# First modulation block split into two halves of 128 channels, context tiles and tables loaded elsewhere, in a one-core diffusion backbone kernel

## Chip, cores and metric

The kernel runs on one core of a Trainium2 chip. The metric is the device time of one execution in microseconds (us), lower is better. All data is float32; the large matrix products take their operands as pairs of a rounded part and a remainder ("H" and "L" tiles) and add three products of them.

## What is computed

Two layers over 256 latent tokens `x` and 256 context tokens `ctx`, with 2048 channels each. The part that matters here is the entry of the first layer: every token row is normalised, then scaled and shifted by vectors that come from a matrix product with the conditioning vector, and the result is multiplied with the columns of the input projection.

```python
def rms_norm(x, g):
    y = x * rsqrt(mean(x * x, -1) + 1e-6)
    return y * g
m = silu(cond) @ ada_w + ada_b            # 2048 -> 3 * 2048
shift, scale, gate = split(m, 3)
h  = rms_norm(x,   g) * (1 + scale)   + shift      # latent rows, cond = c
hc = rms_norm(ctx, g) * (1 + scale_c) + shift_c    # context rows, cond = c_ctx
p, pc = h @ w_in, hc @ w_in[:, keys and later]     # q, gates, z, k, v, xBC, dt
# then neighbourhood attention + two-way state space scan, output projection,
# residual with the gate; second layer: the same kind of entry, a gated short
# convolution between two projections, residual with its gate
```

## The kernel before

The program is one long instruction list. It is written out while a planner (class `Plan`, lines 38 to 133) keeps an estimated finishing time for each engine and tile; generators hand in pieces of work, and `pump` (278) and `force` (299) decide from these estimates which piece is written next. On the chip each engine then runs its instructions strictly in that order. `pump` looks through the lists `urgent`, `side` and `back`, takes the first task in the list that `may` go (246), and starts again from the top of the list, so that in `urgent` a task that was spawned earlier goes first as long as its turn is possible.

Weights come in chunks of 128 x 1024 (512 KB) through a set of raw buffers: five named `raw`, and during the entry four more (`PT` twice, `xtm`, `yi`; line 181). `loads` is the fixed order of the loads, all issued on SyncE's queue by `issue` (365) as raw buffers come free. A chunk is rounded on ScalarE (line 420) and its remainder taken on VectorE (line 427) into one of three places; `use` and `used` hand these to the matrix products.

The entry has eight blocks of 256 channels, j = 0 to 7. For each block `ada_gen` (702) computes scale and shift: four 512 KB chunks of `ada0` for each of the two, 16 matmuls of 128 x 256 for each (line 718), a copy to SBUF (724), two transposes (728), a reduction and one or two small additions on VectorE (732 to 738). Then the two 128-channel tiles of normalised, transposed tokens (`xm`) are turned into `hH` (ScalarE, 757) and `hL` (VectorE, 759 and 763). For block 0 the weight chunk of the keys is rounded in two halves by `split_half` (436), one for each channel tile. Tokens are loaded by `x_load` (578), 128 rows at a time: t = 0 and 1 are latent rows, t = 2 and 3 context rows. Rows 2 and 3 go into the tiles `KT` and `KL`, in which rows 0 and 1 stood before. `x_norm` (594) computes the row sums and scales the rows; `x_pair` (617) transposes two channel tiles and copies them out of PSUM, one on ScalarE (628), one on VectorE (629). `x_gen(0)` is the first task in `urgent`, `ada_gen` the second, `x_gen(1)` the third.

The main loop (870) starts with block 0: keys of t = 0, 1 (12 matmuls for both channel tiles), then values (12), then queries (12), then keys and values of t = 2 and of t = 3, then the B columns (`b_part`). Blocks 1 to 7 follow in the same way, for all rows at once. `rows_` and `kv` (848, 859) issue these products.

Two tables, the rest of `small` (170 KB) and of `const` (224 KB), are loaded right after the context rows (lines 533, 534). `gemv_gen` (812), on the list `back`, computes further modulation vectors on VectorE from `adaT` chunks; it needs the conditioning vector as a row broadcast to all partitions, in the tile `csb`. Its loads share the raw buffers from the end of the entry on (`later_loads`, 505).

Of the kernel before, what the change touches and what calls it, by code (L numbers as in the profile page):

```python
# [14 lines left out]
D = 2048  # L15
KB = 16
# [125 lines left out]
def kernel(ctx: ExitStack, tc, x, cx, ada0, w0, adaT, w_in, w_out, sc_in, sc_out, rpb, small, const,  # L142
# [32 lines left out]
    QT, Vt, gt = st([128, 4, 256], "QT", F32R), st([128, 4, 512], "Vt"), st([128, 4, 256], "gt")  # L175
    xrow.append(st([128, D], "KL", name="x1"))
    QL = st([128, 4, 256], "QL", F32R)
# [351 lines left out]
    q_ada(0)  # L529
    w_seg(0, CK, CV, CQ)  # L530
    loads.append(lambda: x_load(2))
    loads.append(lambda: x_load(3))
    loads.append(lambda: E(DMA.dma_start(sm[:, NFIRST:], small[:, NFIRST:])))
    loads.append(lambda: E(DMA.dma_start(cs_[:, CFIRST:], const[:, CFIRST:])))
    weight(w_in, 0, 2, COL_B, 256)
    q_ada(1)
    for j in range(1, 8):
        w_seg(j, CK, CV)
        if j < 7:
            q_ada(j + 1)  # L540
        w_seg(j, CQ)
        weight(w_in, j * 256, 2, COL_B, 256)
    loads.append(later_loads)
# [31 lines left out]
    XS = {}  # L575
    ssq = st([128, 16], "ssq")

    def x_load(t):
        src = x if t < 2 else cx
        r0 = (t % 2) * 128  # L580
        xt = xrow[t] if t < 2 else st([128, D], ("KT", "KL")[t % 2], name=f"x{t}")
        for q in range(0, 4, 2):
            E(DMA.dma_start(xt[:, q * 512:(q + 2) * 512], src[r0:r0 + 128, q * 512:(q + 2) * 512]))  # L583
            XS[4 * t + q], XS[4 * t + q + 1] = (xt[:, p * 512:(p + 1) * 512] for p in (q, q + 1))

# [47 lines left out]
    def x_gen(c):  # L633
# [6 lines left out]
        for k2 in range(c, KB // 2):  # L640
            yield from x_pair(k2, ts)
# [60 lines left out]
    def ada_gen():  # L702
        bc = lambda ap: ap.unsqueeze(2).to_broadcast([128, 2, 2])
        for j in range(8):
            k2 = slice(2 * j, 2 * j + 2)
            for part, dst in ((0, A0), (1, S0)):
                ps = None
                for q in range(4):
                    key = ("ada", j, part, q)
                    w_ = 2 if j == 0 else 4  # L710
                    if q % w_ == 0:
                        ks = [("ada", j, part, q + i) for i in range(w_)]
                        yield when(lambda: all(k in RAW for k in ks))
                        yield W_("PE", *[RAW[k][1] for k in ks], nb=0 if ps is not None else 1)
                    if ps is None:
                        ps = bank()
                    raw, v = RAW.pop(key)
                    for g in range(4):
                        mm(ps[32 * g:32 * g + 32, :256], cpad[:, 4 * q + g, :], v[:, g, :], q == 0, q == 3)
                    give_raw(raw)  # L720
                    issue()
                yield W_("ACT", ps)
                Rt = half()
                E(S.copy(Rt, ps[:, :256]))

                yield W_("PE", Rt)
                for b in range(2):
                    turn(ps[:, 256 + b * 128:384 + b * 128], Rt[:, b * 128:(b + 1) * 128])
                give(free_h, Rt)
                yield W_("DVE", ps)  # L730
                p2 = dst[:, k2, :]
                E(V.tensor_reduce(out=p2, in_=ps[:, 256:].rearrange("p (b g c) -> p b c g", b=2, c=32)[:, :, 0:2, :],
                                  axis=AX.X, op=ALU.add))
                if part == 0:
                    E(V.tensor_tensor(out=dst[:, k2, :], in0=p2, in1=bc(bs1[:, k2]), op=ALU.add))
                    E(V.tensor_tensor(out=dst[:, k2, :], in0=dst[:, k2, :], in1=bc(g0[:, k2]), op=ALU.mult))
                else:
                    E(V.tensor_tensor(out=dst[:, k2, :], in0=p2, in1=bc(P_("ab0")[:, k2]), op=ALU.add))
                give(free_b, ps)

            for ts in ((0, 1), (2,), (3,)) if j == 0 else ((0, 1, 2, 3),):
                yield when(lambda: all(("xm", t, j) in got for t in ts))
                spans = [(k, slice(max(256 * k, 128 * ts[0]), min(256 * k + 256, 128 * ts[-1] + 128)))
                         for k in range(2) if {2 * k, 2 * k + 1} & set(ts)]
                o = slice(128 * ts[0], 128 * ts[-1] + 128)
                for kb in (2 * j, 2 * j + 1):
                    if j:

                        yield when(lambda: need[0] >= j or plan.t["DVE"] <= plan.t["PE"] + 600)
                    yield W_("DVE", xnT[kb][:, o])  # L750
                    hf = tmp()
                    if hH[kb] is None:
                        hH[kb] = st([128, 512], f"hH{kb}", F32R, name=f"hH{kb}")
                    if ts == (0, 1):
                        split_half(kb)
                    for k, ok_ in spans:
                        E(S.activation(hH[kb][:, ok_], xnT[kb][:, ok_], AF.Identity, scale=A0[:, kb, k:k + 1],  # L757
                                       bias=S0[:, kb, k:k + 1]))
                        E(V.tensor_scalar(out=hf[:, ok_], in0=xnT[kb][:, ok_], scalar1=A0[:, kb, k:k + 1],
                                          scalar2=S0[:, kb, k:k + 1], op0=ALU.mult, op1=ALU.add))  # L760
                    if hL[kb] is None:
                        hL[kb] = st([128, 512], f"hL{kb}", F32R, name=f"hL{kb}")
                    E(V.tensor_tensor(out=hL[kb][:, o], in0=hf[:, o], in1=hH[kb][:, o].bitcast(F32), op=ALU.subtract))  # L763
                    give(free_t, hf)
                    if ts == (0, 1):
                        halfsplit.pop()()
                if ts == (0, 1):
                    hold[0] = False
                    split()
                    split()  # L770
                got.update(("h", j, t) for t in ts)
# [26 lines left out]
    rowt = st([128, 128], "rowt")  # L798
    n_back = [0]
# [12 lines left out]
    def gemv_gen():  # L812
        yield from rows_out(csil[:, 0:KB], crow[0])
# [1239 lines left out]
```

## Time and profile before

| what | value |
|---|---|
| time, median of 3 runs | 1763.3 us (1760.74 to 1771.8) |
| time of the profiled execution | 1760.31 us |
| its span, first to last instruction | 1758.5 us |
| TensorE busy | 1736.7 us, 99% of the span |
| VectorE busy | 1223.6 us, 70% |
| ScalarE busy | 773.4 us, 44% |
| granted TensorE clock, mean | 0.999 |
| moved by DMA | 377.66 MB, mean 215 GB/s |

The profile lists busy time by engine, by group of instructions and by window of time; PE is TensorE, PEld its weight load, DVE VectorE, ACT ScalarE, POOL GpSimd, SPq the queue of SyncE that issues the loads. A timeline row gives start, duration, engine, line, operation, tiles and count, and in brackets how long the engine had been idle and what ended that. "Idle" of TensorE is what decides here, since it is busy nearly all the time.

### The profile page before, as it was taken

What the parts mean: (1) busy time and instruction counts of PE and PEld (TensorE: products, weight loads), DVE (VectorE), ACT (ScalarE), POOL (GpSimd) and SP (SyncE); (2) the same over time, 40 slices, a digit from 0 to 9 for tenths busy, and PEclk for the clock granted to TensorE, in tenths of its full rate; (3) what the DMA queues carried; (4) which work ended last, traced back from release to release, by engine and by line L of the source; (5) the groups of instructions that cost most, each with busy time, mean ns of one, the idle gap of its engine ahead of it and who ended that gap; (6) DMA issues with size and microseconds to landing.
All of it is one profiled execution on the core that took longest, in us unless ns stands there. A gap on an engine that the chain in (4) does not pass through costs nothing.

```text
span 1758.5 us, 25025 instructions
## 1 busy us (share of the span) xinstructions
PE 1736.7 (99%) x9451; PEld 1463.1 (83%) x9451; DVE 1223.6 (70%) x1978; ACT 773.4 (44%) x1330; POOL 31.6 (2%) x28
## 2 busy tenths in 40 slices
PE   6999999999999999999999999999999999999998
PEld 4777988889888889888888898888888888888887
DVE  5666887878685878686877787787668555555554
ACT  5333544445242436343435343564446444444442
POOL 0000100001000000000000000000000000000000
PEclk9999999999999999999999999999999999999999
DMA  9987644686756767656776557768767666666563
GB/s 362 342 307 258 209 143 138 183 246 191 234 165 195 219 205 227 210 175 210 220 213 193 166 185 255 246 221 284 274 222 228 195 188 192 192 191 188 190 208 121
DMA packets 202536, 377.66 MB, mean 215 GB/s; under 512 B 32384, under 2 KB 69040, under 8 KB 202416
## 3 DMA queue, kind: packets, MB, share of 16 engines
q1 hardware_dynamic: 195152, 369.49, 65.5%
q10 hardware_dynamic: 7264, 6.58, 1.1%
q8 instruction: 74, 1.21, 0.3%
q14 instruction: 46, 0.38, 0.1%
HBM read 370.62 MB, written 6.71 MB: 215 GB/s over the span
## 4 chain that ended last, share of the span: by engine, by line
PE 94%; DMA 2%; DVE 2%; issue 1%; ACT 0%; POOL 0%; SPq 0%; ACTq 0%; DVEq 0%; POOLq 0%
PE bank L195 91%; PE bank L199 3%; DMA tmp<-dram_csr 1%; DVE w L427 1%; DMA raw<-in_ada 0%; DMA tmp<-dram_exr 0%; DMA raw<-in_adaT 0%; DVE tmp L1235 0%; ACT w L420 0%; POOL statk L572 0%; DVE mix L1562 0%; SPq L583 0%; DVE raw L823 0%; DVE tmp L603 0%; DVE Vt L1012 0%
## 5 line engine op out<-in xcount | busy, mean ns | idle before, releaser
L420 ACT CAST w<-raw 128x1024 fp32r<-128x1024 f32 x343 | 359.5, 1049 | 530.4 <-PE bank L195 447.7
L427 DVE TENSOR_TENSOR w<-raw,w 128x1024 fp32r<-128x1024 f32 x343 | 416.6, 1217 | 231.4 <-ACT w L420 230.1
L195 PE MATMUL bank<-hH,w 128*128 128x256 f32 (+1 forms) x2064 | 488.0, 324 | 1.2 <-DVE w L427 1.1
L195 PE MATMUL bank<-w,hH 128*128 128x512 f32 x1280 | 407.4, 396 | 2.7 <-ACT hH L757 2.5
L195 PEld LDWEIGHTS bank<-hH,w 128*128 128x128 f32 x2064 | 344.7, 188 | 34.2 <-DVE w L427 2.1
L195 PE MATMUL bank<-hL,w 128*128 128x256 f32 (+1 forms) x1040 | 334.3, 321 | 0.0
L195 PEld LDWEIGHTS bank<-w,hH 128*128 128x128 f32 x1280 | 237.7, 189 | 54.4 <-issue 4.0
L195 PE MATMUL bank<-w,hL 128*128 128x512 f32 x640 | 249.9, 391 | 0.1
L195 PEld LDWEIGHTS bank<-hL,w 128*128 128x128 f32 x1040 | 196.3, 189 | 14.9
L195 PE MATMUL bank<-w,h 128*128 128x512 f32 x768 | 179.7, 390 | 0.0
L823 DVE CUSTOM_DVE_ANT_0 raw<-raw,csb 128x1024 f32<-128x1024 f32 x128 | 155.4, 1219 | 26.2 <-DMA raw<-in_adaT 24.0
L195 PEld LDWEIGHTS bank<-w,h 128*128 128x128 f32 x768 | 143.6, 188 | 29.6
L195 PEld LDWEIGHTS bank<-w,hL 128*128 128x128 f32 x640 | 120.5, 188 | 25.4 <-DVE hL L763 0.6
L195 PE MATMUL bank<-w,mix 128*128 128x512 f32 x588 | 138.3, 391 | 0.9 <-DVE w L427 0.9
L195 PEld LDWEIGHTS bank<-w,mix 128*128 128x128 f32 x588 | 109.5, 188 | 24.0 <-DVE w L427 1.3
L1235 DVE SCALAR_TENSOR_TENSOR tmp<-bank,cwh,tmp 128x508 f32<-128x508 f32 (+1 forms) x96 | 71.0, 744 | 1.8
L195 PE MATMUL bank<-KL,h 128*128 128x512 f32 x264 | 63.8, 389 | 0.0
L427 DVE TENSOR_TENSOR KL<-raw,KL 128x1024 fp32r<-128x1024 f32 x32 | 39.1, 1223 | 33.1 <-ACT KL L420 33.1
L427 DVE TENSOR_TENSOR wL<-raw,wH 128x1024 fp32r<-128x1024 f32 x31 | 37.9, 1224 | 33.5 <-ACT wH L420 33.4
L427 DVE TENSOR_TENSOR QL<-raw,QT 128x1024 fp32r<-128x1024 f32 x32 | 39.2, 1224 | 29.8 <-ACT QT L420 29.8
L195 PEld LDWEIGHTS bank<-KL,h 128*128 128x128 f32 x264 | 49.5, 188 | 10.2
L195 PE MATMUL bank<-QT,h 128*128 128x512 f32 x168 | 56.2, 391 | 0.0
(291 smaller groups left out, 1984.7 us busy)
## 6 DMA issues: line engine op xcount, KB each, us to landing
raw<-in_w_in SPq DMA_DIRECT2D x196, 512.0 KB, 3.9
raw<-in_adaT SPq DMA_DIRECT2D x128, 512.0 KB, 4.8
raw<-in_sc_in SPq DMA_DIRECT2D x128, 512.0 KB, 3.8
raw<-in_w_out SPq DMA_DIRECT2D x64, 512.0 KB, 5.0
raw<-in_ada SPq DMA_DIRECT2D x34, 512.0 KB, 6.9
raw<-in_sc_out SPq DMA_DIRECT2D x32, 512.0 KB, 4.1
PT<-in_ada SPq DMA_DIRECT2D x16, 512.0 KB, 6.9
raw<-in_w SPq DMA_DIRECT2D x16, 512.0 KB, 6.1
```

Of the source, the lines that this page charges most:

```text
L195: E(T.matmul(o, l, r, start=start, stop=stop, skip_group_check=True))
L199: E(T.transpose(o, i, ident if k == 128 else ident[:k, :k]))
L420: E(S.copy(H, v))
L427: E(V.tensor_tensor(out=Lo, in0=v, in1=H.bitcast(F32), op=ALU.subtract))
L823: E(V.tensor_tensor_reduce(out=raw, in0=raw, in1=csb, scale=1.0, scalar=0.0, op0=ALU.mult, op1=ALU.add, accum_out=gp[:, h, m:m + 1]))
L1235: E(V.scalar_tensor_tensor(out=do, in0=di, scalar=cwh[:, 32 * k + ch:32 * k + ch + 1], in1=do, op0=ALU.mult, op1=ALU.add))
```

## The change

Block 0 is cut into its two 128-channel tiles. Its eight `ada0` chunks are repacked on the host so that four of them hold all that channel tile 0 needs and four all that tile 1 needs (each chunk is now 8 x 128 rows by 128 columns). Their loads stand around the key and value chunks: four for tile 0, keys, values, four for tile 1, queries. The matmuls for them are 128 x 128, 64 in place of 32 of 128 x 256. The main loop issues keys and values of tile 0 as soon as tile 0 is modulated, then waits for tile 1 and issues the rest.

The transposes of the latent rows beyond the first pair (`x_pair` with k2 from 1) wait until the transposed shift of tile 1 has been written out (`("mm", 1, 1)`).

Context rows go to places that are free from the start: row tile 2 to `QT` and `QL`, row tile 3 to `csb` and to `hH14` and `hH15`. As `csb` is taken until then, `gemv_gen` starts only when the entry is over (`("V", 0)`). The two tables are loaded after block 3's chunks. `split_half` now enters the key chunk as split after its first half, and gives the raw buffer back after the second.

```diff
+    xhalf = [st([128, 1024], "QT", name="x2a")]
+    xhalf.append(st([128, 1024], "QL", name="x2b"))
...
             if b:
                 RAW.pop(0)
+                give_raw(raw)
+                issue()
+            else:
                 place()
                 HL[0] = (H, Lo)
                 pos["split"] += 1
-                give_raw(raw)
-                issue()
...
-    q_ada(0)
-    w_seg(0, CK, CV, CQ)
+    def q_ada_one(kb):
+        for part in range(2):
+            for q in range(2):
+                loads.append(("a", ("one", kb, part, q), ada0, 4 * kb + 2 * part + q, 8, 0, 128, 2))
+
+    q_ada_one(0)
+    w_seg(0, CK, CV)
+    q_ada_one(1)
+    w_seg(0, CQ)
     loads.append(lambda: x_load(2))
     loads.append(lambda: x_load(3))
-    loads.append(lambda: E(DMA.dma_start(sm[:, NFIRST:], small[:, NFIRST:])))
-    loads.append(lambda: E(DMA.dma_start(cs_[:, CFIRST:], const[:, CFIRST:])))
...
+        if j == 3:
+            loads.append(lambda: E(DMA.dma_start(sm[:, NFIRST:], small[:, NFIRST:])))
+            loads.append(lambda: E(DMA.dma_start(cs_[:, CFIRST:], const[:, CFIRST:])))
...
+        if t < 2:
+            ps_ = [xrow[t][:, :1024], xrow[t][:, 1024:]]
+        else:
+            ps_ = xhalf if t == 2 else [csb, *xlast]
...
         for k2 in range(c, KB // 2):
+            if k2 == 1 and not c:
+                yield when(lambda: ("mm", 1, 1) in got)
             yield from x_pair(k2, ts)
...
+        def part_sum(part, kbs, keys, together):
+            n = 128 * len(kbs)
+            nb, ps = 1024 // n, None
+            for q in range(len(keys)):
+                if q % together == 0:
+                    ks = keys[q:q + together]
+                    yield when(lambda: all(k in RAW for k in ks))
+                    yield W_("PE", *[RAW[k][1] for k in ks], nb=0 if ps is not None else 1)
+                if ps is None:
+                    ps = bank()
+                raw, v = RAW.pop(keys[q])
+                for g in range(nb):
+                    ki = q * nb + g
+                    mm(ps[32 * (g % 4):32 * (g % 4) + 32, :n], cpad[:, ki, :], v[:, g, :], ki < 4, ki >= 12)
...
+            for b in range(len(kbs)):
+                turn(ps[:, 256 + b * 128:384 + b * 128], Rt[:, b * 128:(b + 1) * 128])
+            got.add(("mm", kbs[0], part))
+            give(free_h, Rt)
+            yield W_("DVE", ps)
...
+        for kb in range(2):
+            for part in range(2):
+                yield from part_sum(part, (kb,), [("one", kb, part, q) for q in range(2)], 1)
+            yield both((0, 1), 0)
+            yield from rows_of(0, kb, (0, 1))
+            got.add(("row", kb))
+            if kb == 0:
+                split()
+        hold[0] = False
+        split()
...
     def gemv_gen():
+        yield when(lambda: ("V", 0) in got)
         yield from rows_out(csil[:, 0:KB], crow[0])
...
-        force(lambda: ("h", j, 0 if j == 0 else 3) in got, (urgent,))
+        force(lambda: ("h", j, 3) in got if j else ("row", 0) in got, (urgent,))
         if j == 0:
-            w3 = [use(k) for k in range(3)]
-            psQ = banks(2)
-            psk = banks(2)
-            for k in range(2):
-                for i, (a_, w_) in enumerate(((hH, 0), (hL, 0), (hH, 1))):
-                    for t in range(2):
-                        mm(psk[t], a_[k][:, t * 128:(t + 1) * 128], w3[0][w_][:, k], k == 0 and i == 0, k == 1 and i == 2)
-            for t in range(2):
-                spawn(urgent, part_gen(j, "K", t, parK[t], psk[t]))
-            pump()
-            for t in range(2):
-                kv(j, "V", t, w3[1])
+            w3, pss0 = [], []
+            for k in range(2):
+                if k:
+                    force(lambda: ("h", 0, 1) in got, (urgent,))
+                for q, (key, par) in enumerate((("K", parK), ("V", parV))):
+                    if k == 0:
+                        w3.append(use(q))
+                        pss0.append(banks(2))
+                    for i, (a_, w_) in enumerate(((hH, 0), (hL, 0), (hH, 1))):
+                        for t in range(2):
+                            mm(pss0[q][t], a_[k][:, t * 128:(t + 1) * 128], w3[q][w_][:, k], k == 0 and i == 0, k == 1 and i == 2)
+                    pump()
+                    if k:
+                        for t in range(2):
+                            spawn(urgent, part_gen(j, key, t, par[t], pss0[q][t]))
+                        pump()
+            w3.append(use(2))
+            psQ = banks(2)
             for t in range(2):
                 rows_(j, "Q", t, psQ[t], w3[2], True, False)
```

More of the change, by code (lines that the diff above doesn't have):

```diff
@@ L702, in ada_gen @@
     def ada_gen():
[L703 to L771, printed above, removed]
@@ new lines, in ada_gen @@
+        both = lambda ts, j: when(lambda: all(("xm", t, j) in got for t in ts))
+        for kb in range(2):
[8 more added lines that the diff above has]
+        split()
+        got.update(("h", 0, t) for t in (0, 1))
+        for t in (2, 3):
+            yield both((t,), 0)
+            for kb in range(2):
+                yield from rows_of(0, kb, (t,))
+            got.add(("h", 0, t))
```

74 lines of the change are left out of this document (67 added, 7 removed).

## The prediction

> **What bounds the kernel now.** I read the page first (span, then the chain that ended last), then the busy time by windows, then TensorE's waits.
>
> ```profile
> span 1758.5 us, 25025 instructions
> PE 94%; DMA 2%; DVE 2%; issue 1%; ACT 0%; POOL 0%; SPq 0%; ACTq 0%; DVEq 0%; POOLq 0%
> ```
>
> ```profile
> 0.00:10.00 10.00, 0.00 (x0) 0.00 (x0) 4.29 (x17) 4.43 (x9) 0.76 (x5) 1.00 0.77 277
> 10.00:20.00 10.00, 8.56 (x82) 5.66 (x86) 5.61 (x17) 5.67 (x15) 0.56 (x1) 1.00 1.03 414
> 20.00:30.00 10.00, 8.39 (x49) 5.76 (x42) 7.12 (x17) 7.19 (x14) 0.17 (x1) 0.83 1.03 401
> 30.00:40.00 10.00, 8.25 (x44) 5.99 (x46) 4.95 (x15) 6.73 (x17) 1.44 (x4) 1.00 1.01 403
> 40.00:50.00 10.00, 10.00 (x107) 7.19 (x95) 6.76 (x22) 6.26 (x18) 0.00 (x0) 1.00 0.81 311
> 50.00:1700.00 1650.00, 1647.44 (x8951) 1394.05 (x8952) 1168.57 (x1865) 727.64 (x1248) 28.69 (x18) 1.00 0.67 213
> 1700.00:1758.50 58.50, 54.04 (x239) 44.43 (x237) 26.31 (x27) 15.50 (x15) 0.00 (x0) 1.00 0.44 147
> ```
>
> ```profile
> PE bank L195 <- DMA raw<-in_ada: 10.8, 1, 10.8
> ```
>
> The window columns after the stretch and its length are PE, PEld, DVE, ACT, POOL (busy us), then clock, DMA share and GB/s. TensorE is the bound: from 50 to 1700 us it idles 1650.00 - 1647.44 = 2.6 us. Its idle time lies at the start: 10.0 + 1.44 + 1.61 + 1.75 = 14.8 us before 40 us. There the DMA share is 1.0 at over 400 GB/s, so the loads set the pace, and TensorE's one long wait is for the first `ada0` chunk. All that the change can win is in these 14.8 us, less than the 17.6 us that are 1% of the time, which is about what a measurement of this kernel can tell from no change.
>
> I therefore follow one number: when TensorE has done block 0's 36 latent matmuls (keys, values, queries). What follows is the same work.
>
> **The landing of the loads.**
>
> ```profile
> 9.42 0.33 SPq L381 DMA_DIRECT2D xtm<-in_ada  x1
> 10.71 0.33 SPq L381 DMA_DIRECT2D yi<-in_w  x1
> 17.37 1.77 SPq L583 DMA_DIRECT2D x<-in_cx  x4
> ```
>
> ```profile
> xtm<-in_ada SPq DMA_DIRECT2D x1, 512.0 KB, 10.2
> yi<-in_w SPq DMA_DIRECT2D x1, 512.0 KB, 10.2
> ```
>
> ```profile
> 3.50 8.47 DMA raw<-in_ada
> 23.35 10.21 PE bank L195 x36
> 1671.73 82.32 PE bank L195 x363
> ```
>
> The second fence gives KB and us from issue to landing of the first fence's two issues; the third is the chain. After four x loads the `ada0` chunks are the 5th to 12th load. The 6th lands at 3.50 + 8.47 = 11.97, the 12th at 9.42 + 10.2 = 19.6, the keys (13th) at 20.9: 1.28 us a load. In the new order the last chunk of tile 0 is the 8th: 14.5. Keys 15.8, values 17.1, tile 1's four chunks 18.4 to 22.2 (14th), queries 23.5.
>
> **First half.** The tail from the last chunk's matmuls to the first product:
>
> ```profile
> 13.03 4.36 PE L199 MATMUL bank<-const,x 128*128 128x128 f32 x32
> 20.57 0.61 PE L195 MATMUL bank<-xtm,cpad 128*32 128x256 f32 x8
> 21.68 0.44 PE L199 MATMUL bank<-const,half 128*128 128x128 f32 x2 [0.49 <-ACT half L724]
> 23.35 0.74 PE L195 MATMUL bank<-w,hH 128*128 128x512 f32 x2 [1.11 <-ACT hH L757]
> 60.90 1.93 PE L195 MATMUL bank<-raw,cpad 128*32 128x256 f32 x32
> ```
>
> ```profile
> 15.21 3.05 DVE L629 COPY xm<-bank 128x256 f32<-128x256 f32 x7 [0.20 <-ACT xm L628]
> 22.23 0.17 DVE L732 TENSOR_REDUCE S<-bank 128x4 f32<-128x16 f32 x1 [2.23 <-PE bank L199]
> ```
>
> The tail is 23.35 - 20.57 = 2.78 us, so the first product starts at 14.5 + 2.8 = 17.3, 6.0 earlier. A warm matmul takes 82.32/363 = 0.227 us; 12 of them (keys, values of tile 0) end at 20.0. This gain is only kept if the second half comes as early too.
>
> **Second half, the step that decides.** Its last chunk lands at 22.2. From the chunk's first matmul to the end of the transposes of its sum is 21.68 + 0.44 - 20.57 = 1.55 us: 23.75. At this instant ("mm", 1, 1) is set, and 28 transposes of x are let go. `x_gen(0)` is first in `urgent`, ahead of `ada_gen`, and its conditions (a bank, its sources, ScalarE at hand) hold pair after pair, so I read the code as writing out all seven pairs, with their copies on ScalarE and VectorE, before the shift's reduction on VectorE. The 28 take 28 x 4.36/32 = 3.8 us: 27.55. VectorE's last copy ended 15.21 + 3.05 - (13.03 + 4.36) = 0.87 us behind the transposes: 28.4. From the reduction to the first product is 23.35 - 22.23 = 1.12: 29.55. Then 24 matmuls x 0.227 = 5.4: 35.0. Before, the 36 ended at 23.35 + 10.21 = 33.6. **Term: +1.4.** The transposes, which used to run while TensorE waited for chunks, now stand in the way, and the 6.0 us are gone.
>
> **The clock.**
>
> ```profile
> 24.00:25.00 1.00, 1.00 (x5) 0.60 (x4) 0.90 (x3) 1.00 (x2) 0.00 (x0) 0.82 0.98 393
> 25.00:26.00 1.00, 1.00 (x4) 0.81 (x3) 1.00 (x3) 1.00 (x2) 0.00 (x0) 0.50 1.05 418
> 28.00:29.00 1.00, 1.00 (x6) 0.83 (x5) 1.00 (x4) 0.92 (x2) 0.00 (x0) 0.97 1.05 384
> ```
>
> From about 24.8 to 28.0 TensorE was granted half its clock, after a stretch in which it waited much; the 36 matmuls took 10.21 instead of 36 x 0.227 = 8.2, a loss of 2.0 us. In the new order the same loss on tile 0's products would be covered by the wait until 22.2. But a new idle stretch of 2.0 us (27.55 to 29.55) stands before the other 24. Ends 0 and +2.0; nothing places it, so I take +1.0.
>
> **The context rows.**
>
> ```profile
> 33.40 0.38 PE L199 MATMUL bank<-const,x 128*128 128x128 f32 x2
> 35.13 0.50 PE L195 MATMUL bank<-w,hH 128*128 128x512 f32 x1 [1.36 <-ACT hH L757]
> 38.82 0.87 PE L199 MATMUL bank<-const,x 128*128 128x128 f32 x6 [0.31 <-ACT x L613]
> ```
>
> Their normalisation is still written behind tile 1's modulation, so these 5.4 us move with it. After it the new order has less to round (values are done) but also less time: 0 to +1.0, I take 0. That the rows no longer wait for the old tiles (issued at 17.37, when loads were on the way until 23.5, the 15th at 1.28 each) lets them land about a microsecond sooner; they were not what was waited for: 0. Their one more DMA costs SyncE 1.77/4 = 0.44: 0 to +0.4, I take 0, since that queue is paced by the data. The tables (394 KB, 1.0 us of DMA) leave a stretch where no product waited for their successors: 0; block 3's chunks cover them, and without that cover it is the same 1.0.
>
> **Smaller matmuls.** One of 128x256 takes 1.93/32 = 0.06. There are 64 halves for 32, between 0.03 and 0.06 each. All but the last eight wait for chunks anyway; those eight cost 0 to +0.24: +0.1, in the middle.
>
> **The vectors on VectorE.**
>
> ```profile
> L823 DVE CUSTOM_DVE_ANT_0 raw<-raw,csb x128: 1210/1218/1227, 171.1 to 1333.4; 128x1024 f32<-128x1024 f32 x128
> DMA to landing us min/median/max: 4.3/5.8/9.7
> ```
>
> ```profile
> 160.72 0.42 SPq L381 DMA_DIRECT2D raw<-in_adaT  x1
> 189.27 1.30 DVE L789 TENSOR_TENSOR Vt<-Vt,bank 128x512 f32<-128x512 f32 x2
> ```
>
> ```profile
> dram_crow<-rowt ACTq DMA_DIRECT2D x1, 8.0 KB, 5.1
> raw<-in_w_in SPq DMA_DIRECT2D x196, 512.0 KB, 3.9
> raw<-in_w SPq DMA_DIRECT2D x16, 512.0 KB, 6.1
> L420 ACT CAST w<-raw 128x1024 fp32r<-128x1024 f32 x343 | 359.5, 1049 | 530.4 <-PE bank L195 447.7
> L427 DVE TENSOR_TENSOR w<-raw,w 128x1024 fp32r<-128x1024 f32 x343 | 416.6, 1217 | 231.4 <-ACT w L420 230.1
> ```
>
> `gemv_gen` now starts when the entry's values are summed, about 189.27 + 1.30 = 190.6. Then the row (5.1 to landing) and `csb` (at least 4.3): the first of its operations comes at 201 or later, not 171. The work itself can wait, as the 128 chunks run on to 1333. The raw buffers can't: the order of `issue` lets two `adaT` chunks sit in two of five buffers from 160.7 to about 201, and SyncE's weight loads queue behind the wait for the row. Three buffers: a chunk needs 0.4 + 3.9 + 1.05 + 1.22 = 6.6 us, so one is ready every 2.2 us, and TensorE uses one in 12 x 0.227 = 2.7. Cost 0, cover 0.5 us a chunk; ends 0 and +5 (rival C).
>
> **Sum.** +1.4 + 1.0 + 0.1 = +2.5, ends +1.4 and +1.4 + 2.0 + 0.24 + 1.0 + 0.4 = +5.0. The later order is written anew too; idle there is 2.6 + 4.5 us, so I allow 1 us either way. The profiled execution took 1760.31, 1.8 around its span; with +2.5 it is 1762.8. The median shown, 1763.3, lies 3.0 higher; three runs don't say which one a new median follows, so I go half way: **1764**.
>
> **Rivals.**
>
> A, the forecast: transposes ahead of the shift, 1761.7 to 1765.3, 1764 with the offset.
>
> B, the change does what it says: the planner writes the shift's chain first. Then tile 1's first product starts at 22.2 + 2.8 = 25.0 and the 36 end at 30.4, -3.1. The 28 transposes (3.8) then come later, where 1.75 us of idle (30 to 40) take them in part: net -1.1, ends -3.1 and 0: 1759.2, from 1757.2. For it: one failing condition in `may`, a bank or ScalarE not at hand by the planner's own clock, hands the turn to `ada_gen`. Against it: the first pairs were written without a break before (x32 and x7 above), on the same conditions.
>
> C, the raw buffers: if a chunk's cycle is over 3 x 2.7 = 8.2 us, TensorE starves in 160 to 201. With the entry's landing of 6.1 it is 8.8, so 0.2 us for each of 41/2.7 = 15 chunks: +3. With 2 us more in the queues, 0.9 each, +13. About +5 on top of A's 2.5: 1767.8. It passes 1% from a cycle of about 11.7 us. Against it: DMA share is 0.67 on the mean, and the order of loads was already kept by the same rule.
>
> D, the clock is low for all of tile 1's products: then 24 matmuls lose between 2.0 and 5.4 us (24 x 0.227, every one at half speed), on the mean 3.7: +5.1, 1765.4. It decides if transposes leave the clock low. In favour: the 0.50 above followed a stretch with few products. Against: the clock stayed at 1.00 through and after the 32 transposes at 13 us. The Trainium skill, "TensorE: Matmul & The Clock Gate", Part 4, says that transposes don't count as TensorE activity in the usual way, which speaks for D; no row here shows the clock fall behind transposes. By the same page's Part 1, where the clock halves after an idle window of about 3.4 us, a 2.0 us gap would leave it high, and the sum would be +1.5 and the time 1761.8. The trace doesn't agree with that limit as it stands: the half clock came with waits of 1.1 us and less between small pieces of work.
>
> **Chances.** A 0.42, B 0.25, D 0.15, C 0.13, something else 0.05. The range 1757 to 1769 goes from B's low end to C's price with part of the offset and leaves out C's upper part and the rest, under 0.2; A alone spans 1761.7 to 1768.3 (its high end on the median). Faster by over 1% would need more than all the idle time there is: 0.01. Slower by over 1% needs C at its worst: 0.03. Within 1%: 0.96.
>
> **What would show it.** First key product at 17 to 18 us; 28 transposes in one run, then a gap of 1.5 to 2 us, then the products of tile 1 at 29 to 31, and the 36 done at 35 to 37. If the reduction of tile 1's shift stands before the xm copies on VectorE and tile 1 starts at 25, B holds. The first L823 near 201 us, TensorE without gaps between 160 and 230: C is out. A clock of 0.50 after 29 us is for D. I am wrong if the 36 end before 33, or if TensorE idles over 4 us between 50 and 1700.

## The result and the profile after

The changed kernel takes 1771.16 us (median of 22 runs, 1767.43 to 1778.88), the kernel before 1765.19 us (22 runs, 1759.36 to 1772.39). The ratio is 1.0033, 95% interval 1.0021 to 1.0045: 5.8 us slower (0.0033 x 1765), with an interval of 3.7 to 7.9. That is within 1%, as forecast, but 2.2 us above the top of the range (1769), and the loss is more than twice the forecast 2.5.

The profiled execution took 1767.94 us. From the page of the kernel after, its span and the shares of the chain that ended last; then its windows (columns as before the change; the stretch from 50 us on is cut at 65):

```profile
span 1766.2 us, 25159 instructions
PE 92%; DVE 3%; DMA 2%; ACT 1%; issue 1%; SPq 0%; POOL 0%; ACTq 0%; DVEq 0%; POOLq 0%
```

```profile
0.00:10.00 10.00, 0.00 (x0) 0.00 (x0) 3.92 (x15) 4.06 (x8) 0.76 (x5) 1.00 0.76 274
10.00:20.00 10.00, 7.33 (x78) 5.03 (x79) 5.73 (x18) 5.53 (x13) 0.56 (x1) 1.00 1.03 415
20.00:30.00 10.00, 7.31 (x100) 5.42 (x98) 4.23 (x15) 4.33 (x12) 0.00 (x0) 1.00 1.04 401
30.00:40.00 10.00, 8.27 (x33) 6.08 (x34) 7.46 (x22) 7.57 (x19) 0.55 (x1) 0.97 0.93 367
40.00:50.00 10.00, 10.00 (x102) 7.12 (x102) 4.85 (x16) 5.91 (x14) 1.06 (x3) 0.86 0.49 184
50.00:65.00 15.00, 12.93 (x77) 9.09 (x75) 7.79 (x18) 6.50 (x13) 0.00 (x0) 0.89 0.85 303
65.00:1700.00 1635.00, 1632.01 (x8863) 1381.62 (x8862) 1158.97 (x1850) 722.22 (x1240) 28.70 (x18) 1.00 0.67 212
```

The same stretches of the kernel before, where they were not shown:

```profile
50.00:65.00 15.00, 15.00 (x114) 10.63 (x115) 7.75 (x15) 5.21 (x9) 0.00 (x0) 1.00 1.01 378
65.00:1700.00 1635.00, 1632.44 (x8839) 1383.42 (x8838) 1160.82 (x1851) 722.43 (x1240) 28.69 (x18) 1.00 0.67 211
```

From 65 us on TensorE's busy time is the same within 0.4 us. Nearly all of the loss arises before, at two places: up to 30 us, where the forecast looked (1.2 us less busy time between 10 and 20 us, from where the transposes were moved, 1.1 less between 20 and 30), and 50 to 65 us, where TensorE was never idle before and is now idle for 2.1 us, with the clock at 0.89.

The timeline of TensorE in the kernel after (start, duration, line, tiles, count, and in brackets the idle time ahead and what ended it):

```profile
17.94 0.74 PE L196 MATMUL bank<-w,hH 128*128 128x512 f32 x2 [1.15 <-ACT hH L775]
...
24.41 3.75 PE L200 MATMUL bank<-const,x 128*128 128x128 f32 x28
29.99 0.74 PE L196 MATMUL bank<-w,hH 128*128 128x512 f32 x2 [1.82 <-ACT hH L775]
...
35.73 0.38 PE L200 MATMUL bank<-const,x2a 128*128 128x128 f32 x2
37.76 0.51 PE L196 MATMUL bank<-w,hH 128*128 128x512 f32 x1 [1.65 <-ACT hH L775]
...
50.79 0.38 PE L200 MATMUL bank<-const,half 128*128 128x128 f32 x2
...
55.78 0.39 PE L196 MATMUL bank<-w,hH 128*128 128x512 f32 x1
...
58.46 0.49 PE L196 MATMUL bank<-w,hH 128*128 128x512 f32 x1 [2.07 <-DVE w L428]
58.89 0.64 PE L196 MATMUL bank<-PT,cpad 128*32 128x256 f32 x8
```

The first four rows are the forecast's story: first product at 17.94, the 28 transposes in one run, a gap of 1.82, block 0's 36 latent products done at 35.9 instead of 33.6. VectorE's timeline of the kernel after shows why: the copies of the transposed tokens, of which this is the last, stand ahead of the reduction of tile 1's shift.

```profile
28.61 0.42 DVE L646 COPY xm<-bank 128x256 f32<-128x256 f32 x1 [0.27 <-ACT xm L645]
28.95 0.15 DVE L752 TENSOR_REDUCE S<-bank 128x2 f32<-128x8 f32 x1
```

The last four rows of TensorE's fence are the part that was not foreseen. At 50.79 the shift of block 1 is transposed; from then on block 1's tokens have to be rounded before its first products can run. TensorE has the last context products, the B columns, and two of block 1's products that were ready. At 56.4 it runs out and waits until 58.46. ScalarE's timeline and VectorE's show the chain it waits for:

```profile
51.62 1.09 ACT L775 ACTIVATE hH<-xm,S,A 128x256 fp32r<-128x256 f32 x2 [0.42 <-DVE S L758]
52.62 0.56 ACT L825 COPY gt<-bank 128x512 f32<-128x512 f32 x1
53.08 1.05 ACT L421 CAST w<-raw 128x1024 fp32r<-128x1024 f32 x1
54.03 1.04 ACT L421 CAST w<-PT 128x1024 fp32r<-128x1024 f32 x1
54.98 0.58 ACT L825 COPY Vt<-bank 128x512 f32<-128x512 f32 x1
55.46 1.09 ACT L775 ACTIVATE hH<-xm,S,A 128x256 fp32r<-128x256 f32 x2
```

```profile
56.58 0.69 DVE L781 TENSOR_TENSOR hL<-tmp,hH 128x512 fp32r<-128x512 f32 x1 [2.30 <-ACT hH L775]
57.19 1.22 DVE L428 TENSOR_TENSOR w<-raw,w 128x1024 fp32r<-128x1024 f32 x1
```

The second half of the tokens is rounded (55.46) behind two casts and two copies, its remainder behind that (VectorE idles 2.30 for it), and the remainder of the key chunk last. From the transposes to the end of this row it is 57.19 + 1.22 - 50.79 = 7.6 us, for which TensorE had 56.4 - 50.79 = 5.6 us of work. In the kernel before, the same span of TensorE's timeline is full:

```profile
45.52 0.38 PE L199 MATMUL bank<-const,half 128*128 128x128 f32 x2
45.74 1.04 PE L199 MATMUL bank<-const,x 128*128 128x128 f32 x8
46.53 0.48 PE L195 MATMUL bank<-w,hH 128*128 128x512 f32 x1
...
49.37 0.39 PE L195 MATMUL bank<-hH,w 128*128 128x512 f32 x1
...
52.43 1.07 PE L195 MATMUL bank<-PT,cpad 128*32 128x256 f32 x16
...
54.30 0.50 PE L195 MATMUL bank<-w,hH 128*128 128x512 f32 x1
```

Transposes of context rows (45.74), all products of the last token tile (46.53), the B columns (49.37), block 2's first sums (52.43): 54.30 - 45.52 = 8.8 us of work and no wait. Of block 1's products only the third needs the key chunk's remainder, as the row at 58.46 shows in the kernel after; in the kernel before the third stands at 54.87, so the cover that compares with the 5.6 us is 54.87 - 45.52 = 9.4. In the kernel after the transposes and three of the products have run before the shift is ready, and the sums (58.89) stand behind the wait. That the chain was hardly shorter before shows in VectorE's row for the remainders of block 1's two chunks:

```profile
51.33 2.36 DVE L427 TENSOR_TENSOR w<-raw,w 128x1024 fp32r<-128x1024 f32 x2
```

The first of the two ends at about 51.33 + 2.36/2 = 52.5, 7.0 us behind the shift's transposes and only 2.4 us ahead of the product at 54.87 that needs it.

Two rows of one-microsecond windows of the kernel after, one from each stretch of half clock (39.4 to 42.9 and 60 to 63.4 us; the kernel before has one such stretch, about 24.7 to 28.0). Summed over windows of 1 us, length x (1 - clock) is 1.7 us for each of the three:

```profile
40.00:41.00 1.00, 1.00 (x3) 0.72 (x3) 0.34 (x2) 0.88 (x2) 0.91 (x3) 0.50 0.10 29
60.00:61.00 1.00, 1.00 (x16) 0.44 (x8) 0.00 (x0) 0.00 (x0) 0.00 (x0) 0.50 0.86 283
```

### The profile page after: what moved, and what is told of

The parts are those of the page before. It is cut to its first block, busy times and chain, and to the rows that moved or that the text cites. A ratio compares the mean times of both kernels' runs of the same rounds, so it can differ in the third digit from the quotient of the medians.

```text
span 1766.2 us, 25159 instructions
## 1 busy us (share of the span) xinstructions
PE 1739.4 (98%) x9515; PEld 1465.0 (83%) x9515; DVE 1225.5 (69%) x1983; ACT 774.1 (44%) x1332; POOL 31.6 (2%) x28
## 4 chain that ended last, share of the span: by engine, by line
PE 92%; DVE 3%; DMA 2%; ACT 1%; issue 1%; SPq 0%; POOL 0%; ACTq 0%; DVEq 0%; POOLq 0%
PE bank L196 89%; PE bank L200 3%; DVE w L428 1%; DMA tmp<-dram_csr 1%; DMA raw<-in_ada 0%; ACT w L421 0%; DMA raw<-in_w_in 0%; SPq L1089 0%; DVE mix L1612 0%; DMA raw<-in_sc_in 0%; DVE tmp L1285 0%; DVE raw L867 0%; ACT hH L775 0%; POOL statk L582 0%; DVE tmp L1454 0%
## 5 line engine op out<-in xcount | busy, mean ns | idle before, releaser
L421 ACT CAST w<-raw 128x1024 fp32r<-128x1024 f32 x339 | 354.7, 1046 | 530.9 <-PE bank L196 452.8
L428 DVE TENSOR_TENSOR w<-raw,w 128x1024 fp32r<-128x1024 f32 x339 | 411.0, 1215 | 230.1 <-ACT w L421 228.9
L867 DVE CUSTOM_DVE_ANT_0 raw<-raw,csb 128x1024 f32<-128x1024 f32 x128 | 155.8, 1220 | 29.8 <-DMA raw<-in_adaT 29.7
```

Of the source, the lines that this page charges most:

```text
L421: E(S.copy(H, v))
L428: E(V.tensor_tensor(out=Lo, in0=v, in1=H.bitcast(F32), op=ALU.subtract))
L867: E(V.tensor_tensor_reduce(out=raw, in0=raw, in1=csb, scale=1.0, scalar=0.0, op0=ALU.mult, op1=ALU.add, accum_out=gp[:, h, m:m + 1]))
```

## The experiments

Theory (cover): what is lost beyond the transposes is lost at block 1, since the written order leaves too little TensorE work behind block 1's shift. Rivals: the transposes ahead of tile 1 explain the loss; the half clock does, and waits only choose its place; the transfers of the added weights do.

**Undoing the gate, or one part alone.** e1 lets the 28 transposes go one step later, e2 takes the gate away, e3 has the split block and the gate, with the places, the tables and `gemv_gen` as before the change, e4 the free places, late tables and late `gemv_gen` with the block whole.

```diff
# e1, on the changed kernel
-                yield when(lambda: ("mm", 1, 1) in got)
+                yield when(lambda: ("row", 1) in got)
# e2, on the changed kernel
-            if k2 == 1 and not c:
-                yield when(lambda: ("mm", 1, 1) in got)
# e3, on the changed kernel: context rows back to the old tiles
+        xt = xrow[t] if t < 2 else st([128, D], ("KT", "KL")[t % 2], name=f"x{t}")
...
# e4, on the kernel before
+            ps_ = xhalf if t == 2 else [csb, *xlast]
...
+        yield when(lambda: ("V", 0) in got)
```

> The changed kernel, but the 28 later transposes wait until tile 1 has been modulated instead of only until its sum is transposed. If the transposes ahead of the shift are the loss: tile 1's first product at about 25 to 26 us instead of 30.0, the 36 latent products done at about 31 to 33 instead of 35.7, and the time 3 to 5 us under the changed kernel's (near 1767). If the loss comes from the moved context rows and the later start of the vectors on VectorE: no change, near 1771. If it comes from what follows in block 1 (rounding of its key weights, half clock): the 36 are done earlier, but the time stays within 2 us of 1771.

Measured 1770.81 us, ratio 1.0037 (1.0024 to 1.0049). TensorE's timeline of e1:

```profile
26.00 1.91 PE L200 MATMUL bank<-const,x 128*128 128x128 f32 x16
27.66 0.71 PE L196 MATMUL bank<-w,hH 128*128 128x512 f32 x2
...
57.61 0.50 PE L196 MATMUL bank<-w,hH 128*128 128x512 f32 x1 [2.78 <-DVE w L428]
```

Tile 1's products now start at 27.66, with no gap, and the 36 are done at 34.7, but the wait at block 1 grows from 2.07 to 2.78 and the time doesn't fall. The transposes alone don't explain the loss; this is the third case of the expectation.

> The changed kernel without the wait of the transposes for tile 1's sum. If the place of the transposes is the loss: they run before 17 us while chunks are awaited, the first product comes at 18 to 21, tile 1's at about 25, the 36 done at 31 to 32, time 4 us or more under the changed kernel's. If the loss is elsewhere: time near 1771.

Measured 1768.25 us, 1.0025 (1.0012 to 1.0038): between the two cases of its expectation. The 36 are done at 33.5, level with the kernel before; a wait of 1.49 us stands before block 1's products at 54.8, and half clock from 55.4 to 58.8.

> The split of block 0 alone: context rows in the old tiles, tables early, vectors on VectorE started early. If the split and its order carry the loss: +4 to +7 us against the kernel before (1769 to 1772). If the moved rows and the late start of the vectors carry it: within 1.5 us of the kernel before.

Measured 1769.68 us, 1.0028 (1.0014 to 1.0043), as expected if the split carries the loss. But its trace shows another loss than that of the kernel after:

```profile
49.83 0.64 PE L195 MATMUL bank<-raw,cpad 128*32 128x256 f32 x8 [0.64 <-DMA raw<-in_ada]
```

The context rows go again where the latent rows stand until the gated transposes have run (25.64 to about 29.4), and the loads behind them wait with them: the context rows are issued at 29.36 instead of 17.37, and between 24 and 28 us nothing is moved. TensorE then waits twice for block 1's `ada0` chunks, 0.64 us each (the second time at 51.11). Behind block 1's shift, from 52.61 to its first product at 61.38, it has 8.8 us of work and no wait. So the missing cover explains the wait at block 1 in the kernel after, e1, e2 and e4, and nothing in e3; and the gate needs the free places.

> The kernel before with the other half of the change: context rows in free places, tables late, vectors started after the entry. If the split carries the loss: within 1.5 us of the kernel before. If raw buffers held by waiting chunks cost time (rival C): +3 to +6 us, with waits of TensorE between 160 and 230 us.

Measured 1767.29 us, 1.0022 (1.001 to 1.0034): slower too, without any split, where at most 1.5 us was expected if the split carried the loss. Rival C isn't the reason: between 160 and 235 us TensorE is busy without a break. TensorE's timeline of e4:

```profile
33.69 0.51 PE L196 MATMUL bank<-w,hH 128*128 128x512 f32 x1 [0.88 <-ACT hH L766]
...
50.01 0.38 PE L200 MATMUL bank<-const,half 128*128 128x128 f32 x2
...
54.64 0.50 PE L196 MATMUL bank<-w,hL 128*128 128x512 f32 x1 [1.98 <-DVE hL L772]
```

The first context product comes at 33.69, 1.4 us ahead of the kernel before (35.13). Then block 1's shift is transposed at 50.01, 4.5 us later than before (45.52): its sums were written behind products of the last token tile and most of the B columns, which used to be its cover. The lead turns into a wait.

**Another pace for the planner, and a first repair.** f5 and f6 change the rate of transfers by which the planner reckons (`RATE = 270.0` to `400.0`) in the kernel after and before. f7 holds some context transposes back until block 1's shift is transposed; f8 is f7 on e1.

```diff
# f7, on the changed kernel
+            if k2 == 1 and c:
+                yield when(lambda: ("mm", 2, 1) in got)
             yield from x_pair(k2, ts)
```

> The changed kernel with one number altered: the planner's load rate 400 in place of 270 (GB/s), the rate that the profile shows in the first 40 us. If the loss beyond the transposes comes from the order, because the planner believes block 1's chunks to land late and writes its sums behind the context rows: block 1's sums move ahead, the wait of TensorE for block 1's first key weights (2.07 us at 58.5) goes, and the time falls by 3 us or more from the changed kernel's 1771. If the loss is the half clock or the moved places: no change within 1.5 us.

> The kernel before with the planner's load rate at 400: the control. If the altered number is good or bad by itself in the later order, it shows here; I expect within 2 us of the kernel before. If it gains as much here as in the changed kernel, then the number, and not the meeting of number and change, is what matters.

Measured 1799.78 us, 1.0206 (1.0189 to 1.0222), and 1809.21 us, 1.0256 (1.0235 to 1.0277). The order of the whole program is written anew and waits appear far behind the entry, up to 7.2 us. Both expectations failed, and these two tell nothing about block 1.

> The changed kernel, with the later transposes of the context rows held back until block 1's second sum is transposed: the same order question by hand, at that place alone. If block 1's late sums are the loss: TensorE's wait at 58.5 goes or shrinks under 1 us and the time falls by 1.5 to 3 us. If not: block 1's first product is no earlier than the 55.8 of the changed kernel, and the time stays near 1771 or rises.

> Both corrections of order by hand: latent transposes behind tile 1's modulation, context transposes behind block 1's sums. If the two losses are separate they add: about 2 us from the first and 2 from the second, near 1766 to 1767. If the first only moves the wait to block 1, the second sets it free and the sum is 4 us or more.

Measured 1769.52 us, 1.0035 (1.0022 to 1.0048), and 1767.55 us, 1.0022 (1.0012 to 1.0033). Misses: the pair held back was block 1's own, so that TensorE now waits 2.28 and 2.49 us for its copies, at 57.73 and 55.19.

**Giving the cover back.** The edit has two parts: block 1's sums come ahead of the last token tile's products, and the context transposes beyond block 1's own pair wait until block 1 is modulated. g9 is this on the changed kernel, g10 on e1, g11 on e2, g12 on e4.

```diff
         for k2 in range(c, KB // 2):
+            if k2 == 2 and c:
+                yield when(lambda: ("h", 1, 3) in got)
...
             for t in range(2, 4):
                 force(lambda: ("h", j, t) in got, (urgent,))
+                if t == 3:
+                    force(lambda: ("mm", 2, 1) in got, (urgent,))
```

> The changed kernel with work held back for block 1: block 1's modulation sums come ahead of the products of the first block's last token tile, and the context transposes beyond block 1's own pair wait until block 1 is modulated, so that TensorE has them to do while block 1's tile is shifted and rounded. Theory (cover): the loss beyond the +2.2 us of the transposes ahead of tile 1 is the wait of 2.07 us at 58.46 us and the half clock behind it, because only 5.0 us of work lay behind block 1's shift transposes where the kernel before had 8.8. Then that wait is below 0.5 us here, there is one half-clock episode instead of two, and the time is 3.5 us under the changed kernel's: 1767 to 1768, a ratio near 1.0015 to the kernel before. Rival (clock): the waits only choose where the half clock falls, there is one such episode wherever the entry waits: the second one moves and the time is within 1 us of 1771. Rival (transfers): block 1's rounded keys are late because of the transfers of the added modulation: the wait stays, 1771.

> The same edit on the version in which the context transposes are let go after tile 1's row is loaded (e1_shift_first, 1770.8 us). Cover: the wait of 2.78 us before block 1's first product goes below 0.5 us and the later products stand within 2 us of the kernel before: about 1766. Rival (clock): within 1 us of 1770.8. Rival (transfers): the wait stays, 1770.8.

> The same edit on the version without the gate on the context transposes (e2_no_gate, 1768.3 us). Cover: the wait of 1.49 us before block 1's first product and the half clock at 55.4 to 58.8 us go: 3 us less, 1765 to 1766. Rival (clock): within 1 us of 1768.3. Rival (transfers): the wait stays, 1768.3.

> The same edit on the version with the free places and the late tables alone, the modulation block whole (e4_places_alone, 1767.3 us), which stood 1.4 to 2.8 us ahead of the kernel before until 52 us. Cover: its waits of 1.98 and 0.48 us at 54.6 and 56.1 us and the half clock at 56 to 59.5 us go, and the lead of 1.4 to 2.8 us is kept: 1761.5 to 1763, faster than the kernel before. Rival (clock): the half clock comes elsewhere, within 1 us of 1767.3. Rival (transfers): the wait stays, 1767.3.

Measured 1766.75 us, 1.0019 (1.0008 to 1.003); 1766.37 us, 1.0019 (1.0008 to 1.0031); 1765.7 us, 1.0011 (0.9999 to 1.0022); 1763.24 us, 1.0001 (0.9989 to 1.0012). The wait before block 1 and the half clock behind it are gone in all four. The gain in the ratio is 0.0014 to 0.0021, or 2.5 to 3.7 us. Each of these gains is uncertain by about 3 us, since two intervals go into it; the four together, 3.0 on the mean, are clear of zero. Transfers are out, as they are the same. g9 to g11 came out close to what was expected; g12 did not: it was to be faster than the kernel before, and is level with it. (Where the expectations of g10, g11, h15 and h16 call the transposes that are gated or let go context transposes, the latent ones are meant; the gate of the changed kernel holds only these.) TensorE's timeline of g12:

```profile
45.27 0.44 PE L200 MATMUL bank<-const,half 128*128 128x128 f32 x2 [0.49 <-ACT half L735]
...
53.71 0.39 PE L196 MATMUL bank<-w,hH 128*128 128x512 f32 x1
```

Again 53.71 - 45.27 = 8.4 us of work behind the shift and no wait. But the copies of both sums now lie open, 0.5 us each. The last four runs put one pair of context transposes behind each sum (h14 on g12, h15 on g11, h16 on g10), and the edit of g9 on the kernel before as a control (h13).

```diff
-            if k2 == 2 and c:
-                yield when(lambda: ("h", 1, 3) in got)
+            if k2 in (2, 3, 4) and c:
+                g_ = ("sum", 2, k2 - 2) if k2 < 4 else ("h", 1, 3)
+                yield when(lambda: g_ in got)
...
+                got.add(("sum", 2 * j, part))
                 yield W_("ACT", ps)
                 Rt = half()
```

> Control: the kernel before with the held-back edit (block 1's sums ahead of the last token tile's products, context transposes beyond block 1's own pair after block 1 is modulated). The kernel before has 8.8 us of work behind block 1's shift transposes and no wait there. Theory (cover): nothing to gain here, and the two copies of block 1's sums lie open as they did with this edit elsewhere (0.49 us twice), so +0.5 to +1.5 us, 1764.4 to 1765.4. Rival (the edit is good for any order): faster than the kernel before by 2 us or more.

> The free places and the late tables with the modulation block whole and the edit graded (g12_cover_places_alone, 1763.2 us, with one pair of context transposes let go behind each of block 1's two sums, the rest after block 1 is modulated). Theory (open copies): the two waits of 0.49 us ahead of block 1's turned sums go and no wait comes back before block 1: 1 us less than there, 1762.2, 1.5 us under the kernel before. Rival (the copies are followed by other waits): the time stays at 1763 to 1764.

> The modulation block in halves without the gate on the context transposes, with the graded edit (g11_cover_no_gate was 1765.7). Theory (open copies): 1 us less, 1764.7. Rival (the halved block itself costs the rest, +1.8 us): within 0.7 us of 1765.7, both waits of 0.49 us gone or not.

> The modulation block in halves with the context transposes let go after tile 1's row is loaded and the graded edit (g10_cover_shift_first was 1766.4). Theory (open copies): 1 us less, 1765.4. Rival (the halved block itself costs the rest, +2.5 us): within 0.7 us of 1766.4, both waits of 0.49 us gone or not.

Measured 1764.2 us, 1.0003 (0.9994 to 1.0012); 1763.2 us, 0.9995 (0.9986 to 1.0005); 1765.25 us, 1.0007 (0.9995 to 1.0019); 1765.87 us, 1.0005 (0.9995 to 1.0015). The control gains nothing, so the edit is no gain by itself: it gives back what the order had lost. With the copies covered (no wait stands ahead of either turned sum in h14, h15 and h16) the idle time falls by 0.8 to 1.0 us, and no version differs from the kernel before beyond its interval. That the time falls by the expected 1 us is not shown: the ratios fall by 0.7, 1.1 and 2.5 us, all within their uncertainty, and h14 to h16 also lie where the rival expected them. None beats the kernel before: h14's -0.0005 has zero in its interval.

**One account for all.** A profile gives TensorE's idle time up to 65 us and, from the granted clock, what half speed cost there: length x (1 - clock), summed over windows of 1 us, since 0.01 of clock is 0.4 us in a window of 40. Windows of before, after, e4, g12 and h16, in this order:

```profile
0.00:40.00 40.00, 25.21 (x165) 17.41 (x169) 21.96 (x65) 24.02 (x53) 2.92 (x10) 0.96 0.96 374
40.00:65.00 25.00, 25.00 (x220) 17.82 (x209) 14.50 (x36) 11.47 (x26) 0.00 (x0) 1.00 0.93 351
```

```profile
0.00:40.00 40.00, 22.91 (x209) 16.53 (x210) 21.34 (x67) 21.48 (x50) 1.87 (x7) 0.99 0.94 364
40.00:65.00 25.00, 22.93 (x176) 16.21 (x175) 12.65 (x34) 12.40 (x26) 1.06 (x3) 0.87 0.70 255
```

```profile
0.00:40.00 40.00, 24.69 (x166) 17.21 (x167) 22.68 (x68) 25.26 (x55) 2.91 (x10) 1.00 0.95 364
40.00:65.00 25.00, 22.14 (x168) 14.73 (x167) 11.94 (x30) 8.57 (x19) 0.00 (x0) 0.93 0.78 284
```

```profile
0.00:40.00 40.00, 24.70 (x156) 17.11 (x156) 21.79 (x64) 24.27 (x52) 2.91 (x10) 0.96 0.94 364
40.00:65.00 25.00, 24.01 (x215) 16.96 (x214) 13.44 (x33) 10.46 (x23) 0.00 (x0) 1.00 0.87 315
```

```profile
0.00:40.00 40.00, 24.68 (x213) 18.15 (x214) 20.79 (x67) 21.33 (x50) 2.32 (x8) 0.96 0.94 365
40.00:65.00 25.00, 24.68 (x213) 17.33 (x215) 15.37 (x36) 11.42 (x25) 0.61 (x3) 1.00 0.82 302
```

For the kernel before: idle 65 - 25.21 - 25.00 = 14.8, clock 1.7, which is one stretch. The others in the same way; the last column is (ratio - 1) x 1764:

| kernel | idle to 65 us | clock | both, against before | measured |
|---|---|---|---|---|
| before | 14.8 | 1.7 | 0 | 0 |
| after | 19.2 | 3.4 | +6.1 | +5.8 |
| e1 | 18.5 | 1.7 | +3.7 | +6.5 |
| e2 | 17.8 | 1.7 | +3.0 | +4.4 |
| e3 | 18.0 | 3.4 | +4.9 | +4.9 |
| e4 | 18.2 | 1.7 | +3.4 | +3.9 |
| f7 | 19.2 | 3.4 | +6.1 | +6.2 |
| f8 | 17.8 | 3.4 | +4.7 | +3.9 |
| g9 | 17.9 | 1.7 | +3.1 | +3.4 |
| g10 | 16.6 | 1.7 | +1.8 | +3.4 |
| g11 | 17.0 | 1.7 | +2.2 | +1.9 |
| g12 | 16.3 | 1.7 | +1.5 | +0.2 |
| h13 | 16.0 | 0 | -0.5 | +0.5 |
| h14 | 15.5 | 0 | -1.0 | -0.9 |
| h15 | 16.2 | 1.7 | +1.4 | +1.2 |
| h16 | 15.6 | 1.7 | +0.9 | +0.9 |

One profiled execution foretells the measured difference within 1.6 us everywhere but for e1 (2.8 off), with an uncertainty of about 2 us on each measured figure. So within that uncertainty the entry holds the difference, as idle time first and as half clock second. Half clock after 65 us is left out: none in before, after, g12, h14, h15 and h16, 1.3 to 6.0 us in the profiles of e3, e4, f7, f8, g9, g10, g11 and h13, and one profile of each can't say how often it comes. Taken over the whole span, the same two terms account for every profile by itself: the span less idle time less clock is 1734 to 1738 us in 17 of the 18, for spans from 1758.5 to 1809.1 (f5 has 1740). Against the rival "the clock alone": from e1 to g10, e2 to g11 and e4 to g12 the clock's share stays at 1.7 us (in the last two the stretch that stood behind block 1's wait is gone, and one stands before 29 us), while the idle time falls by 0.8 to 1.9 and the time by 2.5 to 3.7.

## Why the prediction was wrong

**The landing of the loads and the first half** were right: first product 17.94 for 17.3.

**"Second half, the step that decides"** was right in mechanism and nearly in size: 28 transposes in one run (24.41 to 28.16, forecast 23.75 to 27.55), the copies ahead of the reduction, tile 1 at 29.99 for 29.55, the 36 done at 35.9 for 35.0. So rival B is out. The term is +2.3 instead of +1.4 in the trace: 0.4 of the excess is the later start, 0.5 the 24 products, which took 5.9 us for 5.4. That it is worth 2.3 us in the end was not shown: e1 takes 1.7 us of this idle time back (15.4 before 40 us for 17.1) and g10 has the same order there, yet they are no faster than after and g9.

**The step that failed** is the sentence "What follows is the same work", with its consequence under the context rows ("so these 5.4 us move with it") and the 1 us allowed for a new order. The work is the same, its order is not. The planner writes each queue by estimated times; with the entry's estimates moved, block 1's sums were written later against the products that used to cover its rounding, and the transposes earlier. Nothing but that 1 us priced this. The prediction followed one chain to the end of block 0 and shifted the rest. It should have asked what covers block 1: in the trace of before no wait shows there, because 9.4 us of work hide a chain of 7.0. The slack of 2.4 us was there to be read. Price: 2.1 us idle plus one stretch of half clock, 1.7. g9 is the kernel that the forecast had taken for granted, the changed one without a wait at block 1: it measured +3.4 (1.4 to 5.3) for the forecast's +2.5. And the prediction's own sign of being wrong came: between 50 and 1700 us TensorE idles 2.1 + 3.0 = 5.1 us, over the 4 that it named.

**The clock.** +1.0 was taken, ends 0 and +2.0; measured 3.4 - 1.7 = +1.7, two stretches for one. In the profile of the kernel after, rival D's place was wrong: tile 1's products ran at full clock from 29.99, right behind 28 transposes and a gap of 1.82; the slow stretches struck the first context products and the work behind block 1's wait. But the place is a matter of the execution. Up to the first context product f7 and g9 have the same order on TensorE as the kernel after, and there tile 1's products were struck, from 30.3 us on in f7 and from 34.4 in g9. f7's first two took 1.06 us, against 0.74 above:

```profile
30.15 1.06 PE L196 MATMUL bank<-w,hH 128*128 128x512 f32 x2 [1.82 <-ACT hH L777]
```

So one profile can't rule D out, though a stretch of 1.7 us at that place costs less than the 3.7 that D took. By the Trainium skill, "TensorE: Matmul & The Clock Gate", Part 1, the clock is judged over a free-running window of about 3.4 us, so the place varies from run to run. The trace agrees: the stretches are of one length (24.7 to 28.0, 39.4 to 42.9, 60 to 63.4), and their place differs from execution to execution. The trace doesn't agree with the page's demand for an idle window of that length: no wait ahead of these was longer than 2.1 us.

**Rival C** is out, though the vectors started even later than it took: the first L867 came at 279.6 us, not 201,

```profile
L867 DVE CUSTOM_DVE_ANT_0 raw<-raw,csb x128: 1215/1219/1228, 279.6 to 1398.2; 128x1024 f32<-128x1024 f32 x128
```

and TensorE shows no idle time between 160 and 235 us. Tables, smaller matmuls and the SyncE queue left no wait that could be found.

**Sum.** By the account above the terms are +2.3 us of idle time before 40 us, +2.1 between 40 and 65, +1.7 of clock: +6.1, against a forecast of +1.4, 0 and +1.0, with 0.1 for the smaller matmuls. Of the 7.2 us between 1764 and 1771.16, 3.5 are this loss (6.0 between the medians for 2.5). The other 3.7 are the base: going half way from the one profiled execution to the median of three runs meant a kernel before of 1761.5, and 22 runs put it at 1765.19. Either alone would have left the time inside the range (1761.5 + 6.0 = 1767.5, 1765.19 + 2.5 = 1767.7).

**Open:** whether the split block costs anything of its own. With the cover back, the whole block stands at 0.9995 and the halves at 1.0005 and 1.0007, with intervals of about 0.001 either way. Which part of e4 made the planner write block 1's sums late was not taken apart. And e1 measured 2.8 us more than its account; no run says where they are.

## What to carry to other kernels

Where a planner writes out the order, a change at one place rewrites the order behind it. List for every block after the change which work covers its longest chain, and how much slack that cover has; a chain that shows no wait in the profile may be hidden by two microseconds only. A gain at the start is kept only if the next block can use it: e4 led by 1.4 us at the first context product and lost 3.9 in the end. To test such a loss, move the cover back and leave the suspected change in.

## What the runs showed of the hardware

After a wait of 1.5 to 2.8 us before block 1's products the granted clock fell to 0.50 for about 3.4 us in five of six profiled kernels (after, e2, e4, f7, f8, not e1); in the eight profiles with the edit of g9 or the graded one it never fell between 40 and 65 us. A wait of that size doesn't always bring it: behind the 1.82 us before 29.99 the kernel after ran at full clock, f7 behind the same wait at half. A stretch costs about 1.7 us, nearly as much as the wait ahead of it. And in g9 the first twelve products took 5.4 us (18.20 to 23.6) instead of 3.1 at a recorded clock of 1.00: half speed can pass without a trace in the clock column. So can the first work of an execution: in the kernel before 16 matmuls of 128x256 take 2.28 us at 10.82 and 1.07 at 17.32, both at a recorded 1.00. The first of the 32 transposes behind them are slow too: a window from 14.0 to 14.5 us touches 4 of them, the next half us 7. So the recorded 1.00 at 13 us, which the prediction held against rival D, says less than it seems. In h13, with nothing but transposes on TensorE from 13.23 us, each half us touches 4 or 5 of them from 14 to 17.5 and 7 from 17.5 to 18.5: the speed rises during transposes alone.
